# Eight weight buffers at eight different remainders modulo 512 bytes

## The chip, the core and the metric

The kernel runs on one core of a Trainium2 chip. The metric is the device time of one execution in microseconds. The profile comes from one profiled execution of the same program. Engines are named as the profile names them: PE is TensorE (PEld its weight loads), DVE is VectorE, ACT is ScalarE, POOL is GpSimd, SP is SyncE, which issues most of the DMAs.

## The reference

Two transformer layers over one sequence of 512 tokens of width 1024, all in float32. Layer 0 mixes tokens with dilated sliding-window attention, layer 1 with multi-head latent attention; each mixer is followed by a squared-ReLU MLP of hidden width 4096:

```python
for i in range(DEPTH):                       # DEPTH = 2
    h = rms_norm(x, norm_mix[i])
    if i % 2 == 0:                           # three head groups, dilations 1, 4, 16
        y = dilated_mixer(h, a_w_qkv[0], a_q_gain[0], a_k_gain[0], a_w_o[0])
    else:                                    # low-rank q and kv, rotary part of 64
        y = mla_mixer(h, b_w_in[0], ..., b_w_o[0])
    x = x + y
    h = rms_norm(x, norm_ffn[i])
    a = relu(h @ ffn_w1[i])                  # 1024 x 4096
    x = x + (a * a) @ ffn_w2[i]              # 4096 x 1024
```

Nearly all of the arithmetic is in the products of activations with weight matrices: the q, k and v projection (1024 x 9216), the two output projections, and the four MLP matrices.

## The kernel before, in words

The products run on PE in the type `float32r`, in three parts that keep float32's precision. A weight block of 128 partitions x 1024 elements comes from HBM into a float32 tile (`raw`, `wqs` or a block `b`). ACT writes its rounded half `whi`, DVE writes the remainder `wlo` = block - `whi`. Activations are split in the same way, into `hT`, `asp`, `Ssp` or `cT`. Each product is then high x high, high x low and low x high, accumulated in one PSUM bank.

`whi` and `wlo` are tiles of `[128, 2, 512]`, 4096 bytes in each partition. They come from the pool `wp`, which holds four of each (and three of `raw`), and are given out in turn. A `whi` is free again when its last matmul has read it, so ACT's next split can wait for PE, DVE's for ACT, and PE's next matmul for DVE. Three places make them:

- `load_unit` (L150) for the projections and the first MLP matrix: L157 on ACT, L158 on DVE. Its matmuls are at L185. In the mixers and the projections the halves are the moving operand, 512, 448 or 384 columns wide, and the activations the stationary one; in the first MLP matrix (`up`, L873) slices of 128 columns of the halves are the stationary operand, and the activations `hT_f0` and `hT_f1` move.
- the `split_w` of `v_phase` (L403) for most of the v projection, a 2 x 2 block product with seven products: L406 on ACT, L407 on DVE, matmuls at L421, the halves moving, 384 columns wide.
- the `split_w` of `wino` (L792) for the second MLP matrix, again with seven products: L795 on ACT, L796 on DVE, matmuls at L852, the halves moving, 512 columns wide.

The latent mixer's projections of q and kv (L1032) use `load_unit` too.

Pools are laid out one behind the other in each partition. In the program before, every large tile, and with it each of the eight weight halves, `raw`, `wqs`, `hT`, `asp` and the rest, starts at an address with the remainder 192 modulo 512. Slices of 128 float32 columns are 512 bytes long and keep that remainder.

The order of instructions on each engine comes from the Tile scheduler, which orders the program as it is built.

Of the kernel before, what the change touches and what calls it, by code (L numbers as in the profile page):

```python
# [10 lines left out]
F32 = mybir.dt.float32  # L11
F32R = mybir.dt.float32r
# [5 lines left out]
P = 128  # L18
# [69 lines left out]
def encoder_kernel(ctx: ExitStack, tc: tile.TileContext, x, norm_mix, norm_ffn, a_w_qkv, a_q_gain, a_k_gain,  # L88
# [3 lines left out]
    V, A, G, PE = nc.vector, nc.scalar, nc.gpsimd, nc.tensor  # L92
# [3 lines left out]
    def nm(s):  # L96
        uid[0] += 1
        return f"{s}_{uid[0]}"
# [6 lines left out]
    wp = ctx.enter_context(tc.tile_pool(name="wp", bufs=4))  # L105
    gp = ctx.enter_context(tc.tile_pool(name="gp", bufs=1))
# [13 lines left out]
    ident = ck[:, C_ID:C_ID + P]  # L120
    A.activation(warm, nhalf[:, 0:1], AF.Exp)

    def transpose(o, i):
        PE.transpose(o, i, ident)  # L124

# [13 lines left out]
    def load_raw(src, nk, dims, n):  # L139
        raw = wp.tile([P, 2, 512], F32, tag="raw", name=nm("raw"), bufs=3)  # L140
        dst = raw[:, :nk, :n]
        if dims:
            dst = dst.rearrange("p k (t c) -> p k t c", t=dims)
            for k in range(nk):
                nc.sync.dma_start(dst[:, k], src[:, k])
        else:
            nc.sync.dma_start(dst, src)
        return raw

    def load_unit(src, nk, dims, n, home=None, raw=None):  # L150

        if raw is None:
            raw = load_raw(src, nk, dims, n)
        if home is None:
            home = [wp.tile([P, 2, 512], F32R, tag=t, name=nm(t)) for t in ("whi", "wlo")]
        hi, lo = home
        A.activation(hi[:, :nk, :n], raw[:, :nk, :n], AF.Copy)  # L157
        V.tensor_tensor(lo[:, :nk, :n], raw[:, :nk, :n], hi[:, :nk, :n].bitcast(F32), op=ALU.subtract)  # L158
        return hi, lo, nk
# [54 lines left out]
    def norm_tile(r, src, gain_b, hT, pool, xn_bufs=2, xn_tag="xn"):  # L214

        ss = st.tile([P, 8], F32, tag="nss", name=nm("nss"))
        xn = pool.tile([P, D], F32, tag=xn_tag, name=nm("xn"), bufs=xn_bufs)
        mean_square(xn, src, D, ss[:, 0:1])
        rs = rstd_of(ss[:, 0:1], 1, EPS, "nrs")
        V.scalar_tensor_tensor(xn, src, rs, gain_b, op0=ALU.mult, op1=ALU.mult)  # L220
        for half in range(2):
            tp = tp_p.tile([P, 512], F32, tag="tp", name=nm("tp"))
            for j in range(4):
                transpose(tp[:, j * P:(j + 1) * P], xn[:, (half * 4 + j) * P:(half * 4 + j + 1) * P])
            hi = hT[:, half * 4:half * 4 + 4, 0, r * P:(r + 1) * P]
            lo = hT[:, half * 4:half * 4 + 4, 1, r * P:(r + 1) * P]
            tv = tp.rearrange("p (k t) -> p k t", k=4)
            A.activation(hi, tv, AF.Copy)
            V.tensor_tensor(lo, tv, hi.bitcast(F32), op=ALU.subtract)
# [22 lines left out]
    VH = 3 * DH  # L252
# [54 lines left out]
    def v_phase(vp):  # L307
# [93 lines left out]
        A_OF = {1: of_hT(0, 0), 2: of_hT(0, 1), 4: of_hT(1, 1), 5: of_S(1), 6: of_S(2), 7: of_S(3), 3: of_S(4)}  # L401

        def split_w(x):  # L403
            hi = wp.tile([P, 2, 512], F32R, tag="whi", name=nm("whi"))[:, :, :VH]
            lo = wp.tile([P, 2, 512], F32R, tag="wlo", name=nm("wlo"))[:, :, :VH]
            A.activation(hi, x, AF.Copy)  # L406
            V.tensor_tensor(lo, x, hi.bitcast(F32), op=ALU.subtract)  # L407
            return hi, lo

        def split(p, w, u):  # L410
            parts[p, u] = split_w(w[:, 2 * u:2 * u + 2])
# [343 lines left out]
    def split_a(x, pool):  # L755
        t = pool.tile([P, 4, 2, 256], F32R, tag="asp", name=nm("asp"), bufs=4)
        A.activation(t[:, :, 0], x, AF.Copy)
        V.tensor_tensor(t[:, :, 1], x, t[:, :, 0].bitcast(F32), op=ALU.subtract)
        return t

    def wino(tag, Aq, w, wqs, pool, resid, done=None):

        v = w.rearrange("(k p) c -> p k c", p=P)  # L770
        S = {}
        slots = SLOTS[tag % 4]

        def fetch(slot, key, add=False):

            ki, ni = key
            for u in range(2):
                t = wqs[:, 2 * slot + u]
                src = v[:, 4 * ki + 2 * u:4 * ki + 2 * u + 2, 512 * ni:512 * ni + 512]
                if add:  # L780
                    marks["sum"] = nc.gpsimd.dma_start(t, src, accum_op=ALU.add).ins  # L781
                else:
                    nc.sync.dma_start(t, src)
            return [wqs[:, 2 * slot + u] for u in range(2)]

        def stmp(name, x, y, op):
            if name not in S:
                S[name] = pool.tile([P, 4, 256], F32, tag="S", name=nm("S"), bufs=2)
            V.tensor_tensor(S[name], x, y, op=op)
            return S[name]  # L790

        def split_w(x):  # L792
            hi = wp.tile([P, 2, 512], F32R, tag="whi", name=nm("whi"))
            lo = wp.tile([P, 2, 512], F32R, tag="wlo", name=nm("wlo"))
            A.activation(hi, x, AF.Copy)  # L795
            V.tensor_tensor(lo, x, hi.bitcast(F32), op=ALU.subtract)  # L796
            return hi, lo

        sT, s1, s3, s7 = slots
        b1 = fetch(s1, (0, 0))  # L800
        fetch(sT, (0, 0))
        bT = fetch(sT, (0, 1), add=True)
        b3 = fetch(s3, (1, 1))
        fetch(s7, (0, 1))
        b7 = fetch(s7, (1, 1), add=True)

        def operands(p):
            if p == 5:
                return stmp("c", Aq(1, 0), Aq(1, 1), ALU.subtract), bT
            if p == 1:  # L810
                return Aq(0, 0), b1
            if p == 3:
                stmp("d", S["c"], Aq(0, 0), ALU.subtract)
                return stmp("c", S["d"], Aq(0, 1), ALU.add), b3
            if p == 6:
                return S["d"], fetch(sT, (1, 1), add=True)
            if p == 7:
                return stmp("c", Aq(0, 0), Aq(1, 0), ALU.subtract), b7
            if p == 2:
                return Aq(0, 1), fetch(s1, (1, 0))  # L820
            return Aq(1, 1), fetch(sT, (1, 0), add=True)

        def put(i, n, op, banks):
            for t in range(2):
                sl = resid[:, 2 * i + t, 512 * n:512 * n + 512]
                V.tensor_tensor(sl, sl, banks[t], op=op)  # L826
                if done is not None and p in (2, 4, 6, 7):
                    done(2 * i + t, n)

        banks = {}  # L830
        for p, chain, first, (i, n, op) in ORDER if done is None else ORDER_LAST:
            a, wq = operands(p)
            at = split_a(a, pool)
            if first:
                pl, tg = {"a": (sc_p, "sc"), "b": (tp_p, "tp"), "d": (tp_p, "tp")}[chain]
                if done is not None and chain == "d":
                    pl, tg = acc_p, "acc"
                banks[chain] = [pl.tile([P, 512], F32, tag=tg, name=nm(tg)) for _ in range(2)]
            bk = banks[chain]

            tail = done is not None and p in (7, 4)
            parts = {}
            for u, t in ((0, 0), (1, 0), (0, 1), (1, 1)) if tail else ((0, 0), (0, 1), (1, 0), (1, 1)):
                if u not in parts:
                    parts[u] = split_w(wq[u])
                hi, lo = parts[u]
                for j in range(2):
                    k = 2 * u + j
                    ah = at[:, k, 0, t * P:(t + 1) * P]
                    al = at[:, k, 1, t * P:(t + 1) * P]  # L850
                    for i_, (lt, rt) in enumerate(((ah, hi), (ah, lo), (al, hi))):
                        PE.matmul(bk[t], lhsT=lt, rhs=rt[:, j], start=(first and k == 0 and i_ == 0),  # L852
                                  stop=(k == 3 and i_ == 2), skip_group_check=True)
            put(i, n, op, bk)
# [96 lines left out]
    if True:  # L951
        with tc.tile_pool(name="bpool", bufs=1, reuse_waits="tile") as bp, \
# [208 lines left out]
            for s_ in range(HB * NT + lag):  # L1161
                p, c = divmod(s_, 8)
# [64 lines left out]
```

## Time and profile before

| what | value |
|---|---|
| time, median of 2 runs (1428.57 and 1428.98) | 1428.78 us |
| span of the profiled execution, first to last instruction | 1425.8 us |
| granted PE clock over the span | 1.000 |
| PE busy | 1394.0 us (98%) |
| PEld busy | 1183.8 us (83%) |
| DVE busy | 939.6 us (66%) |
| ACT busy | 740.5 us (52%) |
| POOL busy | 217.2 us (15%) |
| mean DMA rate | 130 GB/s |

The timed runs are 3.0 us above the profiled span: that lies around the first and the last instruction. In a group's row, busy time counts overlapping instructions once, and the mean of one is the length of one from its start to its modelled end. Matmuls follow each other faster than that mean, since one starts before the one ahead of it has ended; the distance of their starts is read from a run of them with its count and length, in the chain of waits.

### The profile page before, as it was taken

How to read it: one execution, taken by the hardware profiler on the slowest of the kernel's cores; microseconds unless marked ns; L12 is line 12 of the kernel's file. 1: busy time of each engine (PE TensorE's matmuls, PEld its weight loads, DVE VectorE, ACT ScalarE, POOL GpSimd, SP SyncE). 2: the span in 40 equal slices, each digit the busy share in tenths (PEclk: the TensorE clock that was granted, in tenths of full speed). 3: DMA queues.
4: the chain of work that ended last, by engine and by line, in shares of the span. 5: the costliest groups of instructions: out<-in, count | busy, mean ns of one | idle time of the engine just before them, and what ended most of it. 6: DMA issues, size and time to landing. Idle time of an engine off the chain costs nothing.

```text
span 1425.8 us, 19234 instructions
## 1 busy us (share of the span) xinstructions
PE 1394.0 (98%) x7044; PEld 1183.8 (83%) x7044; DVE 939.6 (66%) x1497; ACT 740.5 (52%) x1594; POOL 217.2 (15%) x240
## 2 busy tenths in 40 slices
PE   7999999999999999999999999999999999999998
PEld 7999888988888988888888887777768888888886
DVE  6886768676886754465564759788745365575647
ACT  6554656464564623553545446677633553544543
POOL 1110212021112001020010203433201020020201
PEclk9999999999999999999999999999999999999999
DMA  9535222322322335668493844200115658394835
GB/s 323 166 134 168 75 87 87 107 89 75 118 61 77 121 134 195 174 133 222 116 233 99 206 120 91 82 31 30 44 40 163 183 127 231 93 234 128 192 90 118
DMA packets 121086, 185.25 MB, mean 130 GB/s; under 512 B 8416, under 2 KB 58336, under 8 KB 120992
## 3 DMA queue, kind: packets, MB, share of 16 engines
q1 hardware_dynamic: 101808, 144.96, 31.6%
q0 software_dynamic: 19184, 39.07, 15.2%
q8 instruction: 55, 0.90, 0.3%
q14 instruction: 39, 0.32, 0.1%
HBM read 176.13 MB, written 7.86 MB: 129 GB/s over the span
## 4 chain that ended last, share of the span: by engine, by line
PE 89%; DVE 6%; ACT 2%; issue 1%; DMA 1%; POOL 0%; SPq 0%; DVEq 0%; ACTq 0%; POOLq 0%
PE acc L185 51%; PE sc L852 11%; PE tp L852 7%; PE tp L124 4%; PE sc L421 3%; PE acc L1138 1%; PE sc L1032 1%; PE acc L1114 1%; PE tp L421 1%; DVE wlo L796 1%; PE sco L701 1%; PE sc L587 1%; PE acc L421 1%; PE sco L697 1%; DVE wlo L407 1%
## 5 line engine op out<-in xcount | busy, mean ns | idle before, releaser
L185 PE MATMUL acc<-whi,hT 128*128 128x512 f32 (+2 forms) x1216 | 384.2, 390 | 2.2 <-ACT hT L739 1.3
L185 PE MATMUL acc<-hT_f,whi 128*128 128x512 f32 (+1 forms) x1152 | 318.7, 366 | 1.7 <-DVE resid L915 1.2
L158 DVE TENSOR_TENSOR wlo<-raw,whi 128x1024 fp32r<-128x1024 f32 (+3 forms) x146 | 172.4, 1189 | 180.2 <-ACT whi L157 179.9
L185 PEld LDWEIGHTS acc<-whi,hT 128*128 128x128 f32 x1216 | 225.4, 188 | 42.0 <-ACT hT L739 1.9
L185 PEld LDWEIGHTS acc<-hT_f,whi 128*128 128x128 f32 x1152 | 208.1, 189 | 37.4 <-DVE resid L915 1.6
L185 PE MATMUL acc<-wlo,hT 128*128 128x512 f32 (+2 forms) x608 | 235.9, 388 | 0.0
L157 ACT ACTIVATE whi<-raw 128x1024 fp32r<-128x1024 f32 (+3 forms) x146 | 149.7, 1031 | 161.5 <-PE acc L185 64.1
L796 DVE TENSOR_TENSOR wlo<-wqs,whi 128x1024 fp32r<-128x1024 f32 x112 | 137.9, 1232 | 113.4 <-ACT whi L795 113.4
L185 PE MATMUL acc<-hT_f,wlo 128*128 128x512 f32 (+1 forms) x576 | 204.9, 366 | 0.0
L795 ACT ACTIVATE whi<-wqs 128x1024 fp32r<-128x1024 f32 x112 | 118.8, 1061 | 161.3 <-PE acc L185 65.8
L852 PE MATMUL sc<-whi,asp 128*128 128x512 f32 x512 | 164.9, 390 | 0.8 <-DVE resid L826 0.7
L781 POOL DMA_DIRECT2D wqs<-in_ffn_w_dram x64 | 77.6, 1344 | 546.1 <-DVE wlo L796 362.4
L185 PEld LDWEIGHTS acc<-wlo,hT 128*128 128x128 f32 x608 | 114.4, 188 | 18.7 <-issue 0.2
L185 PEld LDWEIGHTS acc<-hT_f,wlo 128*128 128x128 f32 x576 | 108.5, 189 | 17.4
L852 PE MATMUL tp<-whi,asp 128*128 128x512 f32 x352 | 112.2, 390 | 1.8 <-DVE resid L826 1.8
L852 PEld LDWEIGHTS sc<-whi,asp 128*128 128x128 f32 x512 | 96.1, 188 | 21.4 <-issue 1.5
L132 POOL TENSOR_TENSOR qrs<-rs_v,nhalf 128x4 f32<-128x4 f32 x48 | 58.7, 1228 | 288.8 <-DVE rs_v L129 239.7
L852 PE MATMUL sc<-wlo,asp 128*128 128x512 f32 x256 | 99.6, 389 | 0.0
L137 ACT ACTIVATE junk<-acc 128x128 f32<-128x128 f32 x192 | 53.0, 276 | 56.4 <-PE acc L185 51.4
L852 PEld LDWEIGHTS tp<-whi,asp 128*128 128x128 f32 x352 | 66.1, 188 | 16.4 <-DVE resid L826 2.7
L852 PE MATMUL tp<-wlo,asp 128*128 128x512 f32 x176 | 68.2, 389 | 0.0
L295 ACT ACTIVATE qkT<-tp 128x512 f32<-128x512 f32 x48 | 35.8, 765 | 51.2 <-PE tp L124 50.9
(231 smaller groups left out, 2185.3 us busy)
## 6 DMA issues: line engine op xcount, KB each, us to landing
wqs<-in_ffn_w_dram SPq DMA_DIRECT2D x80, 512.0 KB, 5.1
raw<-in_ffn_w_dram SPq DMA_DIRECT2D x64, 512.0 KB, 4.5
wqs<-in_ffn_w_dram POOLq DMA_DIRECT2D x64, 512.0 KB, 7.5
raw<-in_a_w_qkv_dram SPq DMA_DIRECT2D x96, 256.0 KB, 3.1
b<-in_a_w_qkv_dram SPq DMA_DIRECT2D x24, 384.0 KB, 5.7
vall<-vo POOLq DMA_DIRECT2D x24, 192.0 KB, 2.2
raw<-in_a_w_o_dram SPq DMA_DIRECT2D x8, 512.0 KB, 3.8
raw<-in_b_w_o_dram SPq DMA_DIRECT2D x8, 512.0 KB, 3.7
```

The source lines that it names most:

```text
L124: PE.transpose(o, i, ident)
L132: G.tensor_tensor(out, v[:, :n], nhalf[:, :n], op=ALU.pow)
L137: A.activation(junk, x, AF.Square, scale=1.0 / math.sqrt(dim), accum_out=out)
L157: A.activation(hi[:, :nk, :n], raw[:, :nk, :n], AF.Copy)
L158: V.tensor_tensor(lo[:, :nk, :n], raw[:, :nk, :n], hi[:, :nk, :n].bitcast(F32), op=ALU.subtract)
L185: PE.matmul(accs[o][:, oc], lhsT=lt, rhs=rt, start=(kt == 0 and p_i == 0 and hv == 0), stop=(kt == total - 1 and p_i == 2), skip_group_che ...
L295: A.activation(dst, tv, AF.Copy)
L421: PE.matmul(banks[t][:, :VH], lhsT=lt, rhs=rt[:, j], start=(first and k == 0 and i_ == 0), stop=(k == 3 and i_ == 2), skip_group_check=True)
L781: marks["sum"] = nc.gpsimd.dma_start(t, src, accum_op=ALU.add).ins
L795: A.activation(hi, x, AF.Copy)
L796: V.tensor_tensor(lo, x, hi.bitcast(F32), op=ALU.subtract)
L852: PE.matmul(bk[t], lhsT=lt, rhs=rt[:, j], start=(first and k == 0 and i_ == 0), stop=(k == 3 and i_ == 2), skip_group_check=True)
```

## The change

Each of the eight buffers becomes 96 bytes longer: `wbuf` takes a tile of 1048 elements (4192 bytes) from the same pool and hands out 1024 of them as `[128, 2, 512]`, from element 0 for `whi` and from element 4 (16 bytes) for `wlo`. A new tile `lead` of 256 bytes in the pool `gp`, which lies behind `wp`, is set to zero once; with the eight times 96 bytes it makes 1024 bytes, by which every tile behind them moves, so that these keep their remainder modulo 512. `raw`, `ck`, `hT` and `wqs` lie ahead of the buffers and stay where they are.

In the built program the four `whi` start at the remainders 192, 288, 384 and 480, the four `wlo` at 80, 176, 272 and 368, and all other large tiles at 192 as before. All eight are multiples of 16 bytes; two of them (192 and 384) are multiples of 64, the other six are not.

```diff
+    lead = gp.tile([P, 64], F32, tag="lead", name="lead")
+    V.memset(lead, 0.0)
+
+    def wbuf(tag):
+        n0 = 4 if tag == "wlo" else 0
+        t = wp.tile([P, 1048], F32R, tag=tag, name=nm(tag))
+        return t[:, n0:n0 + 1024].rearrange("p (k n) -> p k n", k=2)
...
         if home is None:
-            home = [wp.tile([P, 2, 512], F32R, tag=t, name=nm(t)) for t in ("whi", "wlo")]
+            home = [wbuf(t) for t in ("whi", "wlo")]
...
         def split_w(x):
-            hi = wp.tile([P, 2, 512], F32R, tag="whi", name=nm("whi"))[:, :, :VH]
-            lo = wp.tile([P, 2, 512], F32R, tag="wlo", name=nm("wlo"))[:, :, :VH]
+            hi = wbuf("whi")[:, :, :VH]
+            lo = wbuf("wlo")[:, :, :VH]
...
         def split_w(x):
-            hi = wp.tile([P, 2, 512], F32R, tag="whi", name=nm("whi"))
-            lo = wp.tile([P, 2, 512], F32R, tag="wlo", name=nm("wlo"))
+            hi = wbuf("whi")
+            lo = wbuf("wlo")
```

On PE, ACT, POOL and SP the same instructions stand in the same order before and after. On DVE one instruction is new. These are the first rows of DVE's program before (`nhalf` is a constant, `nss` the first tile's sum of squares, `b` the first weight block of the v projection):

```order
L1222 UNCONDITIONAL_BRANCH
L117 MEMSET nhalf 128x8
L129 TENSOR_SCALAR rs_v_158<-nss_156 128x1
L361 SCALAR_TENSOR_TENSOR xn_110<-xts,nrs_160,g_mix_3_119 128x1024
L407 TENSOR_TENSOR wlo_164<-b_4_122,whi_163 128x2x384
```

And these of the changed program, whose line numbers are 8 higher behind the new lines:

```order
L1230 UNCONDITIONAL_BRANCH
L117 MEMSET nhalf 128x8
L124 MEMSET lead 128x64
L137 TENSOR_SCALAR rs_v_160<-nss_158 128x1
L369 SCALAR_TENSOR_TENSOR xn_112<-xts,nrs_162,g_mix_3_121 128x1024
L415 TENSOR_TENSOR wlo_166<-b_4_124,whi_165 128x2x384
```

The zeroing of `lead` stands between the constant and the first instruction that waits for data; nothing reads `lead`.

## The prediction

> **What bounds the kernel now.** I read the page's totals first, then a table by stage, the chain of waits, and the groups of instructions by line. The totals say that PE is never long without work:
>
> ```profile
> span 1425.8 us, 19234 instructions
> PE 1394.0 (98%) x7044; PEld 1183.8 (83%) x7044; DVE 939.6 (66%) x1497; ACT 740.5 (52%) x1594; POOL 217.2 (15%) x240
> ```
>
> The table of busy times by stretch shows where the 2% lie. Its columns are length, PE, PEld, DVE, ACT, POOL (busy us and count), the granted PE clock, the DMA share and GB/s. The rows are the dilated mixer behind its v projection, most of the first MLP, the latent mixer, most of the second MLP, and the end.
>
> ```profile
> 135.00:540.00 405.00, 403.26 (x2238) 348.59 (x2237) 285.22 (x564) 215.24 (x720) 59.25 (x49) 1.00 0.31 96
> ...
> 575.00:860.00 285.00, 285.00 (x1265) 236.04 (x1264) 168.88 (x165) 142.77 (x164) 31.50 (x26) 1.00 0.65 161
> 860.00:1085.00 225.00, 214.51 (x1051) 168.74 (x1051) 169.06 (x414) 135.05 (x392) 62.57 (x90) 1.00 0.17 48
> ...
> 1100.00:1380.00 280.00, 280.00 (x1298) 234.56 (x1298) 153.74 (x150) 133.28 (x154) 32.51 (x27) 1.00 0.67 168
> 1380.00:1425.70 45.70, 40.81 (x178) 32.85 (x176) 32.77 (x35) 20.35 (x23) 4.82 (x4) 1.00 0.40 92
> ```
>
> In 565 us of MLP PE has no idle time at all, at full clock, with DVE busy for 169 of 285 us. There only a shorter distance between matmuls can gain time, and only a longer one, or a split of weights late by more than its slack, can lose it. Busy PE is not yet PE at its best, so I need that distance. The chain of waits has long unbroken runs (start, length, line, count); the first here is of the v projection's matmuls, 384 columns wide, the second of the first MLP's, 512 wide:
>
> ```profile
> 113.65 8.50 PE sc L421 x49
> ...
> 742.95 40.57 PE acc L185 x179
> ```
>
> That is 40.57 / 179 = 226.6 ns for 512 columns and 8.50 / 49 = 173.5 ns for 384. The difference of 53.1 ns over 128 columns is 0.415 ns a column, so 512 columns take 212.5 ns and some 14 ns stand beside them in each matmul, the same at both widths. These 14 ns are the only thing in the bound stretches that a change of addresses could take away.
>
> **What the change touches.** Most matmuls that read a weight half are in these eight groups of the page (count, then busy us and mean ns of one; the mean runs to the modelled end, so it is above the distance):
>
> ```profile
> L185 PE MATMUL acc<-whi,hT 128*128 128x512 f32 (+2 forms) x1216 | 384.2, 390 | 2.2 <-ACT hT L739 1.3
> L185 PE MATMUL acc<-hT_f,whi 128*128 128x512 f32 (+1 forms) x1152 | 318.7, 366 | 1.7 <-DVE resid L915 1.2
> ...
> L185 PE MATMUL acc<-wlo,hT 128*128 128x512 f32 (+2 forms) x608 | 235.9, 388 | 0.0
> ...
> L185 PE MATMUL acc<-hT_f,wlo 128*128 128x512 f32 (+1 forms) x576 | 204.9, 366 | 0.0
> ...
> L852 PE MATMUL sc<-whi,asp 128*128 128x512 f32 x512 | 164.9, 390 | 0.8 <-DVE resid L826 0.7
> ...
> L852 PE MATMUL tp<-whi,asp 128*128 128x512 f32 x352 | 112.2, 390 | 1.8 <-DVE resid L826 1.8
> ...
> L852 PE MATMUL sc<-wlo,asp 128*128 128x512 f32 x256 | 99.6, 389 | 0.0
> ...
> L852 PE MATMUL tp<-wlo,asp 128*128 128x512 f32 x176 | 68.2, 389 | 0.0
> ```
>
> Together 1216 + 1152 + 608 + 576 + 512 + 352 + 256 + 176 = 4848 matmuls. One buffer of eight keeps the remainder 192, so about 4848 x 7/8 = 4242 read a moved one.
>
> **PE.** What the move is worth to a matmul is not in the trace directly, since before it every large operand starts at 192. Three things bear on it. First, the same 389 to 390 ns stand for halves that move (L852) and, by line and shape, for halves that are loaded as weights (`hT_f`):
>
> ```profile
> L185 PE MATMUL acc<-whi,hT 128*128 128x512 f32 x1024 | 331.8, 397 | 2.2 <-ACT hT L739 1.3 <-ACT hT L1140 0.7
> L185 PE MATMUL acc<-hT_f,whi 128*128 128x512 f32 x896 | 270.8, 389 | 0.0
> ...
> L580 PE MATMUL sc<-qkT 128*128 128x128 f32 x64 | 12.4, 275 | 0.0
> ...
> L576 PE MATMUL sc<-qkT 128*128 128x128 f32 x64 | 12.3, 274 | 0.0
> ```
>
> Second, the last two rows are the nearest thing to the change. Both use slices of the same tile `qkT` for both operands; at L576 the moving keys start at the same remainder as the queries, at L580 each matmul takes two pieces of 64 keys of which one starts 256 bytes further modulo 512. They take 274 and 275 ns. Third, were PE's two reads to meet at every step of a weight load of 128 columns, the price would be 128 steps of 0.415 ns, 53 ns, and not 14. I take 0 for the gain. Its end is 4242 x 14 ns = 59 us, if all of the 14 ns were such meetings. The loss I take at 0 too. Its end comes from the largest difference between rows of the same shape, 397 against 389 ns in the mixers: 8 ns x 4242 = 34 us, if a start off a multiple of 64 bytes, which six of the eight have, cost as much as whatever lies behind that difference.
>
> The Trainium skill has a figure against me here: "TensorE: Matmul & The Clock Gate", section "Wait — 56ns, not 53.3ns?", gives a fixed cost of about 2.5 ns for each warm matmul beside its columns. This trace disagrees, with 14 ns. If only that page's 2.5 ns were unavoidable and the rest came from addresses, an estimate of 4242 x 11.5 ns = 49 us would be gained, and the sum would be 1380 us.
>
> **DVE and ACT.** They write and read the halves when splitting. If two reads at the same remainder cost DVE anything, an operation with both inputs in SBUF at 192 would be longer than one with its first input in PSUM. They stand side by side in the groups by line and shape, 683 and 685 ns (L285 and L277):
>
> ```profile
> L158 DVE TENSOR_TENSOR wlo<-raw,whi 128x1024 fp32r<-128x1024 f32 x128 | 155.5, 1224 | 177.3 <-ACT whi L157 177.0
> ...
> L277 DVE TENSOR_TENSOR t<-acc,cosg 128x512 f32<-128x512 f32 x48 | 32.9, 685 | 12.0 <-ACT junk L137 7.2 <-PE tp L124 4.6
> L285 DVE TENSOR_TENSOR t<-t,t 128x512 f32<-128x512 f32 x48 | 32.6, 683 | 0.1
> ```
>
> The same view for ACT, and, for the line that splits `wqs` on DVE, its shortest, median and longest instruction:
>
> ```profile
> L795 ACT ACTIVATE whi<-wqs 128x1024 fp32r<-128x1024 f32 x112 | 118.8, 1061 | 161.3 <-PE acc L185 65.8 <-PE tp L852 48.7 <-PE sc L852 26.0
> ...
> L892 ACT ACTIVATE a<-a 128x512 f32<-128x512 f32 x64 | 40.4, 632 | 2.0
> ...
> L796 DVE TENSOR_TENSOR wlo<-wqs,whi x112: 1217/1226/1539, 606.7 to 1412.2; 128x1024 fp32r<-128x1024 f32 x112
> ```
>
> From 512 to 1024 elements DVE goes from 683 to 1224 ns, 1.06 ns for each added element, ACT from 632 to 1061, 0.84 ns; neither slope leaves room for a meeting at every element. So 0 here too. L796 gives the other end: if every split on DVE took the longest 1539 ns in place of 1226, the factor would be 1.26. In the MLPs PE's full stretches above cover it: some 60 splits x 0.31 us = 19 us more on a DVE that is idle for 116 of 285 us. What counts is the part of the chain that runs through splits:
>
> ```profile
> PE acc L185 51%; PE sc L852 11%; PE tp L852 7%; PE tp L124 4%; PE sc L421 3%; PE acc L1138 1%; PE sc L1032 1%; PE acc L1114 1%; PE tp L421 1%; DVE wlo L796 1%; PE sco L701 1%; PE sc L587 1%; PE acc L421 1%; PE sco L697 1%; DVE wlo L407 1%
> ```
>
> Two shares of 1% are about 28 us, and 26% of that is 7 us, at the ends of the v projection and of the MLPs. POOL's accumulating loads wait for L796 as well and would come as much later; they have the same cover.
>
> **The new instruction, and the shift.** The nearest row for zeroing 128x64 is the constant's 128x8, 0.07 us, and DVE then waits for data until 5.65:
>
> ```profile
> 0.80 0.07 DVE L117 MEMSET nhalf<- 128x8 f32 x1 [0.80 <-PEq L1210]
> ...
> 5.65 0.15 DVE L129 TENSOR_SCALAR rs_v<-nss 128x1 f32<-128x1 f32 x1 [4.78 <-ACT xn L137]
> ```
>
> It is free; without that wait it would cost about its own length, 0.1 us. All tiles behind the buffers lie 1024 bytes further at the same remainder; nothing in the trace distinguishes the two places: 0. No DMA reads or writes a weight half, so no transfer changes its shape, and no wait is added to any engine.
>
> **Sum.** 1425.8 us span + 0 (PE) + 0 (splits) + 0 (new instruction, shift) = 1425.8 us, and with the 3.0 us by which the timed runs (1428.57 and 1428.98) lie above the span, 1428.8 us.
>
> **Rivals.**
> *Meetings resolved (faster).* PE's read of moving columns and its weight load now walk in step through addresses of equal remainder; apart, the 14 ns shrink. In full this gives 1428.8 - 59 = 1370 us; 2% is reached from 28.6 us / 4242 = 6.7 ns a matmul. For it speaks that the 14 ns are there at both widths, as a weight load of constant size would have it; against it L576 beside L580, and that 14 ns are no multiple of such a load. A small form of it is possible in the mixers alone: 4.2 us if half of the 8 ns between 397 and 389 went from the 1024 matmuls of that row; 1424.6 us. Chances: 3% for the large form, 5% for the small one.
> *Starts off a multiple of 64 bytes (slower).* Each read of a displaced half takes one fetch more, on PE's moving side at L852 and in the mixers, on its weight side at `up`. At 8 ns this is 1428.8 + 34 = 1463 us; it decides, at +2%, from 6.7 ns. For it speaks only that no row of before has such a start; against it, that all new starts are still multiples of 16 bytes, and that a fetch more for a run of 2048 bytes should cost some single steps of 0.415 ns: two of them on 4242 matmuls are 3.5 us, 1432.3 us. The Trainium skill ("SBUF — State Buffer", section "Specifications (TRN2)") gives lines of 16 bytes, by which no read here touches one line more. No row here shows the size of a line. Chances: 4% for over 2%, 6% for the small form.
> *Slower splits.* Up to 7 us, 1436 us, as worked out above; 2%.
> *The change does not do what it says.* If the padded tiles were rounded up by the allocator to a multiple of 512 bytes, the `whi` would not be displaced; the built addresses speak against it, and the time would be the forecast's. 1%, counted with the forecast.
>
> **Numbers.** The forecast has 80%: 1428.8 us, with its own range of about 1427 to 1431, since the two runs differ by 0.4 us. The small forms (5%, 6%) reach to 1424.6 and 1432.3. The range of 1424.5 to 1433 holds these and leaves out the large forms (3% and 4%) and part of the slower splits. A difference of 2%, 28.6 us, is what I count as faster or slower; all but the two large forms lie within it, so faster 3%, same 93%, slower 4%.
>
> **What would show it.** Right: runs of about 226.6 ns a matmul at L185 and 173.5 ns at L421 (line numbers 8 higher), 389 ns in the groups of L852, 1224 to 1232 ns for the splits on DVE, and no idle PE in the two MLP stretches. The first rival would show as a shorter distance in just those runs; the second as a longer one, with the groups that read no half (L576, L124) as they were. The forecast would be wrong if 14 ns change by over 2 ns (4242 x 2 ns = 8.5 us).

## The result and the profile after

The changed kernel takes 1445.06 us (1443.68 and 1446.43) against 1428.78 us: the ratio is 1.0115, with a 95% interval of 1.0098 to 1.0131. It is slower by 16 us, clear of the measurement and outside the range of the prediction. By the bound of 2% it counts as no change, but the forecast was that nothing moves at all.

The page's totals after:

```profile
span 1441.9 us, 19235 instructions
PE 1411.2 (98%) x7044; PEld 1183.0 (82%) x7044; DVE 939.6 (65%) x1498; ACT 740.0 (51%) x1594; POOL 217.2 (15%) x240
```

The table by stretch of after for two windows that lie wholly in the MLPs (length, PE, PEld, DVE, ACT, POOL as busy us and count, PE clock, DMA share, GB/s):

```profile
600.00:850.00 250.00, 250.00 (x1081) 202.55 (x1080) 143.26 (x141) 118.16 (x135) 29.09 (x24) 1.00 0.66 163
1150.00:1375.00 225.00, 225.00 (x974) 182.47 (x973) 134.93 (x135) 107.50 (x121) 29.10 (x24) 1.00 0.66 163
```

The same two windows of before:

```profile
600.00:850.00 250.00, 250.00 (x1105) 207.01 (x1104) 148.64 (x147) 123.09 (x140) 29.09 (x24) 1.00 0.65 162
1150.00:1375.00 225.00, 225.00 (x995) 186.36 (x994) 131.86 (x132) 106.68 (x120) 29.11 (x24) 1.00 0.68 166
```

In both kernels PE has no idle time there, at full clock. But in the same 250 us PE starts 1081 matmuls in place of 1105. DVE and ACT are as busy as before over the span (939.6 and 740.0 us). So the time went into the matmuls themselves. The groups by line and shape of after show by how much (busy us, mean ns of one; the line numbers are 8 higher than before):

```profile
L193 PE MATMUL acc<-whi,hT 128*128 128x512 f32 x1024 | 335.0, 400 | 2.2 <-ACT hT L747 1.3 <-ACT hT L1148 0.7
L193 PE MATMUL acc<-hT_f,whi 128*128 128x512 f32 x896 | 275.0, 394 | 0.0
L193 PE MATMUL acc<-wlo,hT 128*128 128x512 f32 x512 | 204.0, 399 | 0.0
L193 PE MATMUL acc<-hT_f,wlo 128*128 128x512 f32 x448 | 171.1, 393 | 0.0
L860 PE MATMUL sc<-whi,asp 128*128 128x512 f32 x512 | 167.4, 394 | 0.5 <-DVE resid L834 0.5
L860 PE MATMUL tp<-whi,asp 128*128 128x512 f32 x352 | 113.8, 394 | 1.1 <-DVE resid L834 1.1
L860 PE MATMUL sc<-wlo,asp 128*128 128x512 f32 x256 | 100.7, 393 | 0.0
...
L588 PE MATMUL sc<-qkT 128*128 128x128 f32 x64 | 12.4, 275 | 0.0
```

Two rows that the prediction did not need are, before:

```profile
L185 PE MATMUL acc<-wlo,hT 128*128 128x512 f32 x512 | 202.7, 396 | 0.0
L185 PE MATMUL acc<-hT_f,wlo 128*128 128x512 f32 x448 | 169.1, 389 | 0.0
```

The first MLP matrix's means went from 389 to 394 and 393, the second's from 390 and 389 to 394 and 393, those of the mixers and projections from 397 and 396 to 400 and 399. The keys that read no weight half (L588, L580 before) stay at 275. The second matrix has one more group of 176, which the page gives with 389 before and 393 after. Put together: 896 x 5 + 448 x 4 + (512 + 352) x 4 + (256 + 176) x 4 ns = 11.5 us in the MLPs, and 1024 x 3 + 512 x 3 ns = 4.6 us in the mixers. The sum is 16.1 us, and the spans differ by 1441.9 - 1425.8 = 16.1 us. Means in whole ns make the agreement closer than it deserves: 0.5 ns on the 4176 matmuls of these groups are already 2 us. The smaller groups moved both ways (384 columns mostly longer by 1 to 4 ns, 256 columns shorter by 2) and nearly cancel; no other large term is needed.

The chain of waits shows the distance of the starts. One run each of the v projection (384 columns), the second MLP matrix and the first (512 columns), after:

```profile
113.71 8.58 PE sc L429 x49
...
652.87 5.59 PE sc L860 x24
...
667.02 41.51 PE acc L193 x179
```

41.51 / 179 = 231.9 ns in place of 226.6, and 8.58 / 49 = 175.1 in place of 173.5. Runs of 24 in the second matrix took 5.44 us (226.7 ns) before and take 5.52 to 5.59 us now (230 to 233 ns).

The splits did not change, on DVE and on ACT:

```profile
L166 DVE TENSOR_TENSOR wlo<-raw,whi 128x1024 fp32r<-128x1024 f32 x128 | 155.5, 1224 | 182.2 <-ACT whi L165 178.9 <-PE acc L193 2.8
```

```profile
L803 ACT ACTIVATE whi<-wqs 128x1024 fp32r<-128x1024 f32 x112 | 118.8, 1061 | 162.4 <-PE acc L193 67.2 <-PE tp L860 55.4 <-PE sc L860 28.1
```

The new instruction stands in the timeline where it was expected (start, length):

```profile
0.85 0.11 DVE L124 MEMSET lead<- 128x64 f32 x1
```

### The profile page after: what moved, and what is told of

Same layout as the page of the kernel before. It is cut to its first block, busy times and chain, and to the rows that moved or that the text cites. A ratio compares the mean times of both kernels' runs of the same rounds, so it can differ in the third digit from the quotient of the medians.

```text
span 1441.9 us, 19235 instructions
## 1 busy us (share of the span) xinstructions
PE 1411.2 (98%) x7044; PEld 1183.0 (82%) x7044; DVE 939.6 (65%) x1498; ACT 740.0 (51%) x1594; POOL 217.2 (15%) x240
## 4 chain that ended last, share of the span: by engine, by line
PE 89%; DVE 6%; ACT 2%; issue 1%; DMA 1%; POOL 1%; SPq 0%; DVEq 0%; ACTq 0%; POOLq 0%
PE acc L193 52%; PE sc L860 11%; PE tp L860 7%; PE tp L132 4%; PE sc L429 3%; PE tp L429 1%; PE acc L1146 1%; PE sc L1040 1%; PE acc L1122 1%; DVE wlo L804 1%; PE sco L709 1%; PE sc L595 1%; PE sco L705 1%; PE acc L429 1%; PE sc L1122 1%
## 5 line engine op out<-in xcount | busy, mean ns | idle before, releaser
L193 PE MATMUL acc<-hT_f,whi 128*128 128x512 f32 (+1 forms) x1152 | 322.4, 369 | 1.5 <-DVE resid L923 1.0
L193 PEld LDWEIGHTS acc<-hT_f,whi 128*128 128x128 f32 x1152 | 207.6, 188 | 41.5 <-DVE resid L923 1.4
L803 ACT ACTIVATE whi<-wqs 128x1024 fp32r<-128x1024 f32 x112 | 118.8, 1061 | 162.4 <-PE acc L193 67.2
```

Of the source, the lines that this page charges most:

```text
L193: PE.matmul(accs[o][:, oc], lhsT=lt, rhs=rt, start=(kt == 0 and p_i == 0 and hv == 0), stop=(kt == total - 1 and p_i == 2), skip_group_che ...
```

## The experiments

Every kernel below has the same instructions in the same order on each engine, apart from one to three zeroings of unused tiles; only addresses differ. "Displaced by d" means that the weight halves start d bytes past the remainder of their partners in the matmul (`hT`, `hT_f0`, `hT_f1`, `asp`, `Ssp`, `cT`), which is 192 modulo 512 unless something else is said. Distances come from the chain of waits: a run of 179 matmuls of the first MLP matrix, in which the halves are loaded as weights, and runs of 24 of the second, in which they move.

### The change again, the shift alone, one other remainder, multiples of 64

The first set asked whether the change is the cause at all, and which part of it. `e1_again` is the changed kernel.

> The changed kernel as it is, once more and in turns with the kernel before. Three theories stand. Rhythm: weight loads and moving reads of successive matmuls fall into a fixed rhythm (226.6 ns for 512 columns) when all weight halves start at one remainder, and find none when the start changes from one matmul to the next (231.6 ns in the trace of after). Line: a start off a multiple of 64 bytes costs some steps in each read. Place: not the remainders but the shift of the other tiles by 1024 bytes, or the moment of the runs, made the difference. Rhythm and line: 16 us above before again (ratio 1.011), 231 to 232 ns in the MLPs. Place, if it was the moment: ratio 1.000, 226.6 ns.

```diff
 e2_shift: halves of 4096 bytes, all the shift in lead
-    lead = gp.tile([P, 64], F32, tag="lead", name="lead")
+    lead = gp.tile([P, 256], F32, tag="lead", name="lead")
-        t = wp.tile([P, 1048], F32R, tag=tag, name=nm(tag))
+        t = wp.tile([P, 1024], F32R, tag=tag, name=nm(tag))        # and n0 = 0
```

> All eight halves of 4096 bytes at remainder 192 as before; only the tile lead, of 1024 bytes, is there, so that everything behind the halves is shifted by 1024 bytes as in the change. Rhythm and line: the time of before, ratio 1.000, 226.6 ns for 512 columns. Place, if it was the shift: ratio 1.011, 231 to 232 ns.

```diff
 e3_all288: as e2_shift, with 96 of the 1024 bytes ahead of the halves
+    pre = pp.tile([P, 24], F32, tag="pre", name="pre")             # pool pp lies between raw and the halves
+    lead = gp.tile([P, 232], F32, tag="lead", name="lead")
```

> All eight halves at one other remainder, 288, which is off a multiple of 64; the other tiles as in the change. Rhythm: the same for all halves, so the rhythm stays, ratio 1.000, 226.6 ns, or another fixed distance. Line: eight of eight starts displaced in place of six, 16 x 8/6 = 22 us above before, ratio 1.015, 233 ns. Place (shift): ratio 1.011.

```diff
 e5_mult64: a step of 64 bytes from half to half
-        t = wp.tile([P, 1048], F32R, tag=tag, name=nm(tag))
+        t = wp.tile([P, 1040], F32R, tag=tag, name=nm(tag))        # n0 = 0, lead of 512 bytes
```

> Eight halves at eight different remainders, all multiples of 64 (192, 256, 320, 384, 448, 0, 64, 128); the other tiles as in the change. Rhythm: no rhythm, ratio 1.011, 231 to 232 ns. Line: no start displaced, ratio 1.000, 226.6 ns. Place (shift): ratio 1.011.

| kernel | ratio (95%) | first matrix, 179 | second matrix, 24 |
|---|---|---|---|
| e1_again | 1.0113 (1.0096 to 1.0130) | 41.4 to 41.5 us, 231 to 232 ns | 5.52 to 5.59 us |
| e2_shift | 1.0000 (0.9990 to 1.0009) | 40.57 us, 226.6 ns | 5.44 us, 226.7 ns |
| e3_all288 | 1.0175 (1.0160 to 1.0190) | 41.92 us, 234.2 ns | 5.59 to 5.60 us, 233 ns |
| e5_mult64 | 1.0114 (1.0098 to 1.0129) | 41.4 to 41.5 us, 231 to 232 ns | 5.53 to 5.59 us |

The effect repeats, and the shift alone has none: "place" falls. The multiples of 64 are as slow as the change, so starts off a multiple of 64 are not the cause: "line" falls as well, although its 1.015 for `e3_all288` came nearest to the 1.0175 measured there. That run surprised the "rhythm" theory in its first form. All halves had one start, and yet the kernel was slower than with eight. A rhythm was there, but a longer one, as the chain of `e3_all288` shows:

```profile
658.09 5.59 PE sc L864 x24
672.31 41.92 PE acc L197 x179
```

So it is not enough that successive halves start alike. What was left was the place of the half, by itself or against that of its partner.

### The difference between what moves and what is loaded

PE's weight load for the next matmul runs beside the present matmul. Before, in a stretch of the timeline (start, length), the load and the matmul begin together and the load ends 0.03 to 0.04 us ahead of the next start:

```profile
701.76 0.39 PE L852 MATMUL sc<-whi,asp 128*128 128x512 f32 x1
701.76 0.19 PEld L852 LDWEIGHTS sc<-wlo,asp 128*128 128x128 f32 x1
...
701.98 0.39 PE L852 MATMUL sc<-wlo,asp 128*128 128x512 f32 x1
```

So the two instructions overlap for most of a distance, and the addresses that they read can differ by a constant, which the second set varies. `e6_d64`, `e7_d128` and `e8_d256` are `e3_all288` with another length of `pre`. `e9_world64` displaces everything together:

```diff
 e6_d64, e7_d128, e8_d256
-    pre = pp.tile([P, 24], F32, tag="pre", name="pre")
+    pre = pp.tile([P, 16], F32, tag="pre", name="pre")             # 32 and 64 in the other two
 e9_world64: the kernel before, with 64 bytes ahead of the first large tile
+    lead = cpool.tile([P, 16], F32, name="lead")
     ck = cpool.tile([P, C_KEEP], F32, name="ck")
```

> All eight halves at remainder 256, 64 bytes past the partners (hT, hT_f, asp, Ssp), which stay at 192. The theory is now that the difference of remainders between what moves and what is loaded as weights at the same time sets the rhythm. Relative: a fixed pattern as with the difference of 96 bytes, 228 to 235 ns for 512 columns in both MLP parts, ratio 1.005 to 1.018. Rival, absolute: the place of a read in 512 bytes counts by itself; then the result is the same as in the kernel where everything is at 256.

> All eight halves at remainder 320, the partners at 192, a difference of 128 bytes. Relative, with 512 bytes as the period: a pattern of its own, 228 to 235 ns. If the period were 128 bytes or a divisor of it: 226.6 ns and the time of before.

> All eight halves at remainder 448, the partners at 192, a difference of 256 bytes. Relative, with 512 bytes as the period: a pattern of its own, 228 to 235 ns; with 256 bytes as the period: 226.6 ns and the time of before.

> The kernel before with 64 bytes put ahead of everything but two constants, so that halves, partners, raw tiles and all the rest start at 256 and every difference is 0. Relative: 226.6 ns and the time of before, ratio 1.000, whatever the run with the halves alone at 256 gives. Absolute: the same as that run.

| kernel | displaced by | ratio (95%) | first matrix, 179 | second matrix, 24 |
|---|---|---|---|---|
| e6_d64 | 64 | 1.0083 (1.0053 to 1.0112) | 41.77 us, 233.4 ns | 5.49 to 5.60 us |
| e7_d128 | 128 | 1.0143 (1.0113 to 1.0172) | 41.60 us, 232.4 ns | 5.57 to 5.60 us |
| e8_d256 | 256 | 0.9996 (0.9985 to 1.0007) | 40.57 us, 226.6 ns | 5.44 us |
| e9_world64 | 0, all at 256 | 0.9996 (0.9985 to 1.0008) | 40.57 us, 226.6 ns | 5.44 us |

The rows for the last two are the same to the last digit. The run with the halves 256 bytes past their partners:

```profile
646.98 5.44 PE sc L864 x24
660.81 40.57 PE acc L197 x179
```

and the one in which everything starts at 256:

```profile
648.25 5.44 PE sc L854 x24
662.08 40.57 PE acc L187 x179
```

Halves at 256 cost 12 us when their partners are at 192 (`e6_d64`) and nothing when those are at 256 too (`e9_world64`). So the difference counts, not the place. And it counts modulo 256 bytes, not 512: a displacement of 256 is none.

### Two remainders, one displaced half of three, the engines beside PE, and 32 bytes

```diff
 e10_lo256, e11_lo96: whi as before, a pad of 256 or 96 bytes between the whi and the wlo
+    wl = ctx.enter_context(tc.tile_pool(name="wl", bufs=4))         # behind a pool with the pad
-        t = wp.tile([P, 1024], F32R, tag=tag, name=nm(tag))
+        t = (wl if tag == "wlo" else wp).tile([P, 1024], F32R, tag=tag, name=nm(tag))
 e12_raw96: 96 bytes ahead of raw, 416 between raw and the halves, 512 behind them
+    pre0 = pq.tile([P, 24], F32, tag="pre0", name="pre0")
+    pre = pp.tile([P, 104], F32, tag="pre", name="pre")
 e13_d32: as e3_all288
+    pre = pp.tile([P, 8], F32, tag="pre", name="pre")
```

> whi at 192 as before, wlo at 448: two different remainders modulo 512 that are equal modulo 256, and the address of the halves steps by 256 from one matmul to the next. If the differences count modulo 256 and not modulo 512: 226.6 ns, ratio 1.000. If any change of the remainder modulo 512 between successive matmuls breaks the rhythm: 229 ns or more, ratio above 1.005.

> whi at 192 as before, wlo at 288: one of three matmuls reads a displaced half. If only the read of the displaced half is stretched: a third of what all halves at 288 cost, 25/3 = 8 us, ratio 1.006, with the other two thirds of the matmuls at 226.6 ns. If the phase that one displaced read leaves behind also stretches the ones after it (rhythm): more than a third, up to the 1.011 of the change.

> Halves and partners at 192 as before, the raw tiles alone at 288, so that ACT and DVE read and write at a difference of 96 in every split of load_unit (mixers, projections and first MLP matrix) and PE's two reads keep the difference 0. If PE's two reads meet each other: 226.6 ns everywhere, ratio 1.000. If PE is held up by the accesses of ACT and DVE, whose remainders against each other the change also moved: 231 ns or more in the first MLP matrix and the mixers, ratio 1.007 to 1.011, and 226.6 ns in the second MLP matrix.

> All eight halves at 224, 32 bytes past the partners. With the differences 64, 96 and 128 giving ratios of 1.008, 1.018 and 1.014, no order is seen; rhythm: a pattern of its own, 227 to 235 ns, ratio 1.001 to 1.018. If only differences of 64 bytes or more count: 226.6 ns, ratio 1.000.

| kernel | ratio (95%) | first matrix, 179 | second matrix, 24 |
|---|---|---|---|
| e10_lo256 | 1.0002 (0.9991 to 1.0013) | 40.57 us | 5.44 us |
| e11_lo96 | 1.0114 (1.0080 to 1.0149) | 41.57 us, 232.2 ns | 5.55 us, 231.3 ns |
| e12_raw96 | 1.0000 (0.9989 to 1.0012) | 40.57 us | 5.44 us |
| e13_d32 | 1.0153 (1.0122 to 1.0185) | 41.76 us, 233.3 ns | 5.60 us, 233.3 ns |

`e10_lo256` alternates between two remainders modulo 512 in successive matmuls and costs nothing; that settles 256 as the period of everything seen here. In `e11_lo96` one matmul of three reads a displaced half, and the price is not a third of that of `e3_all288` but nearly two thirds (1.0114 against 1.0175). The matmuls that read the undisplaced `whi` became longer too, as the groups by shape of that run show; before they were at 389 and 390:

```profile
L197 PE MATMUL acc<-hT_f,whi 128*128 128x512 f32 x896 | 275.4, 394 | 0.0
...
L864 PE MATMUL sc<-whi,asp 128*128 128x512 f32 x512 | 167.4, 394 | 0.5 <-DVE resid L838 0.5
```

In the second matrix (L864) what is loaded is always `asp`, so a matmul of `whi` has the difference 0 both to its own weights and to those that are loaded beside it, and its group is longer all the same. So a matmul whose own two reads fit is stretched by what its neighbours left behind. That fits the changed kernel, in which no buffer stands out, the one still at 192 included: the distances in its second matrix, grouped by the four buffers that take turns, average 231 to 232 ns in each group.

`e12_raw96` speaks against the accesses of ACT and DVE: the splits of `load_unit` read and write there at a difference of 96 bytes, and nothing happens. A trace settles it. In `e3_all288` there is a stretch without any instruction on DVE, ACT or POOL (columns as in the tables by stretch above):

```profile
683.10:685.80 2.70, 2.70 (x13) 2.14 (x12) 0.00 (x0) 0.00 (x0) 0.00 (x0) 1.00 0.65 189
```

PE's timeline there, its first and its last matmul of a low half:

```profile
682.91 0.40 PE L197 MATMUL acc<-hT_f,wlo 128*128 128x512 f32 x1
...
685.72 0.39 PE L197 MATMUL acc<-hT_f,wlo 128*128 128x512 f32 x1
```

From the first to the last of these starts there are 12 matmuls in 2.81 us, 234 ns each, as far apart as in the rest. DMAs were under way there (share 0.65). Another stretch of `e3_all288`, in the latent mixer, has none, with the chain's run of matmuls in it:

```profile
1088.05:1099.15 11.10, 11.10 (x49) 8.95 (x48) 4.62 (x7) 2.30 (x4) 1.12 (x2) 1.00 0.00 0
```

```profile
1087.92 11.20 PE acc L197 x48
```

and the same stretch of before:

```profile
1070.45:1081.25 10.80, 10.80 (x49) 8.97 (x48) 4.60 (x7) 2.30 (x4) 1.12 (x2) 1.00 0.00 0
```

```profile
1070.35 10.88 PE acc L185 x48
```

Without a DMA it is 11.20 / 48 = 233.3 ns against 10.88 / 48 = 226.7, the same difference. So neither the other engines nor the transfers are needed for it. What is left are PE's own two reads; no edit here touches a tile in PSUM, where PE writes.

### The sign of the difference

In `e6_d64` the halves stood 64 bytes past their partners. The weights were then 64 past what moved in the first MLP matrix, and 64 short of it in the second. `e15_d192` exchanges the two, since 192 is -64 modulo 256:

```diff
-    pre = pp.tile([P, 16], F32, tag="pre", name="pre")
+    pre = pp.tile([P, 48], F32, tag="pre", name="pre")
```

> All eight halves at 384, 192 bytes past the partners, which modulo 256 is 64 bytes ahead of them. What is loaded as weights then stands to what moves as +64 where the halves move (second MLP matrix) and as -64 where they are the weights (first MLP matrix): the two roles of the run with the halves alone at 256, exchanged. If the difference modulo 256 between the two reads sets the rhythm, the two distances there, 233.3 ns (first matrix) and 230.8 ns (second matrix, mean), change places: 231 in the first, 233 in the second. If the amount of the displacement counts without its sign or only on one operand, they stay as they are there, or take a value of their own. Ratio 1.007 to 1.012 either way.

The ratio was 1.0115 (1.0086 to 1.0145). Runs of `e15_d192`:

```profile
653.39 5.60 PE sc L864 x24
667.59 40.99 PE acc L197 x179
```

and of `e6_d64`:

```profile
649.34 5.49 PE sc L864 x24
663.38 41.77 PE acc L197 x179
```

The first matrix went from 233.4 to 229.0 ns, the second from 228.8 ns, which most of its runs of 24 have in `e6_d64`, to 233.3 in all of them. The places changed as expected, with 229.0 ns where 231 was expected, so the sign of the difference counts: weights 64 bytes past what moves give 233.3 ns in either role. The other value is not equally sharp. It is 229.0 ns in one role and 228.8 ns in the other, but a part of the runs of 24 in `e6_d64` settled at 5.60 us (233.3 ns): at one difference there can be more than one pattern that lasts.

## Why the prediction was wrong

**What bounds it** held: PE without idle time in the MLPs at full clock, and only the distance of the matmuls can move the time. The 226.6 and 173.5 ns were the right numbers to look at, and they are what changed.

**The term for PE was wrong.** It was taken as 0 and measures 16 us, the sum of the groups above. The prediction looked in two directions, a gain from PE's two reads at equal remainders and a loss from starts off a multiple of 64. For the 0 of the loss it gave no reason of its own, only that this one way to it was unlikely. The loss that came belongs to the pair of reads in which the gain was sought, with the sign reversed: of the differences tried, 0, 32, 64, 96, 128 and 192 modulo 256, none gave 512 columns a distance below the 226.6 ns of the difference 0.

The three reasons given for 0 did not show what they were taken for. That 389 ns stood for halves that move and for halves loaded as weights only said that both roles had the difference 0. L576 beside L580 was meant as the nearest row to the change; its displacement was 256 bytes, and `e8_d256` and `e10_lo256` show that just this displacement is none. And the argument from 53 ns a load supposed a meeting at every step of the load; the real price is 2 to 8 ns.

The Trainium skill's figure of 2.5 ns beside the columns ("TensorE: Matmul & The Clock Gate", section "Wait — 56ns, not 53.3ns?") is not reached at any of these addresses: the 14 ns at difference 0 are the least that was seen at 512 columns. They are not a fixed cost either: at 256 columns a difference of 64 leaves some 8 ns beside the columns (114.2 - 256 x 0.415 ns, from the last section). What they consist of stays open.

**The bound held, but mostly by luck.** The end taken from 397 against 389 ns, 8 ns x 4242 = 34 us, held the result, and the range of 1424.5 to 1433 left it out, because 8 ns was given 4% only. But most of these 8 ns are something else. A matmul right behind matmuls of another kind is longer, as the first one here, behind four transposes:

```profile
200.67 0.60 PE L124 MATMUL tp<-ck,t 128*128 128x128 f32 x4
201.03 0.47 PE L185 MATMUL acc<-whi,hT 128*128 128x512 f32 x1
201.34 0.39 PE L185 MATMUL acc<-wlo,hT 128*128 128x512 f32 x1
```

Of the 1024 + 512 matmuls of the two mixer groups in the kernel before, 110 stand in such a place, with a mean of 474 ns; the other 1426 have 391 ns. So only about 2 of the 8 ns are left for what bears on the change, a rhythm that is lost behind a group of transposes and found again some matmuls later. PE's timeline at one such place (start, length):

```profile
186.58 0.60 PE L124 MATMUL tp<-ck,t 128*128 128x128 f32 x4
186.93 0.71 PE L185 MATMUL acc<-whi,hT 128*128 128x512 f32 x2
187.48 0.39 PE L185 MATMUL acc<-wlo,hT 128*128 128x512 f32 x1
187.71 0.86 PE L185 MATMUL acc<-whi,hT 128*128 128x512 f32 x3
188.41 0.39 PE L185 MATMUL acc<-wlo,hT 128*128 128x512 f32 x1
188.64 0.62 PE L185 MATMUL acc<-whi,hT 128*128 128x512 f32 x2
189.09 0.39 PE L185 MATMUL acc<-wlo,hT 128*128 128x512 f32 x1
```

Behind the transposes two matmuls take 0.55 us and the next three 0.70 us (233 ns each); then 0.68 us pass from 188.41 to 189.09 for three (227 ns). In a stream that was otherwise constant to a nanosecond, this was the trace's sign, before the change, that the distance depends on what came before.

**Two counts were off,** without weight for the outcome. Each product reads `whi` twice and `wlo` once, and the buffer that keeps 192 is a `whi`, so 3232 x 3/4 + 1616 = 4040 matmuls read a moved half, not 4242. And DVE makes 28 + 50 = 78 splits in the 285 us of the first MLP's row, not some 60; at 0.31 us each these are 24 us, still less than the 116 us of idle time.

**DVE, ACT, the new instruction and the shift** were right at 0: the splits keep 1224 and 1061 ns, the zeroing took 0.11 us in DVE's wait, and `e2_shift` gives 1.0000.

**The rivals.** "Meetings resolved" had the right place, PE's two reads, and the wrong sign. "Starts off a multiple of 64 bytes" had the right sign and would have given a time of this size at 4 ns a matmul, but its mechanism is refuted by `e5_mult64` and `e6_d64`, in which all starts are multiples of 64 and the time is longer all the same.

**What stays open.** The runs show that the distance follows the signed difference of the two addresses modulo 256, that history carries over (so that one difference can have two distances, as in `e6_d64`), and that neither the other engines nor DMAs are needed for it. That both reads go to the same piece of memory with a period of 256 bytes in a partition is the plain reading, but only argued. Which part of the weight load meets which part of the moving read was not tried, nor differences that are no multiple of 32, apart from those in the changed kernel.

## What to carry to other kernels

Where a kernel is bound by a dense stream of matmuls, the addresses of the two operands are part of its speed: here 512 columns took 226.6 ns when moving and stationary operand started at the same place modulo 256 bytes, and 229 to 234 ns at every other multiple of 32 that was tried, up to 1.8% of the time. Tiles whose sizes are multiples of 256 bytes, laid one behind the other, keep this by themselves; one odd small tile or a padded buffer between two operands is enough to lose it. To see it in a trace, divide the length of an unbroken run of equal matmuls by its count, and compare with another placement. One value throughout is no proof of a good one: `e3_all288` had 234.2 ns in its runs of 179, as steady as the 226.6 ns of before. In the changed kernel runs of 24 varied from 5.52 to 5.59 us, where before all took 5.44.

## What was not expected of the hardware

- The distance of matmuls depends on the difference of the two addresses modulo 256 bytes, with its sign, and on nothing else about the addresses that was tried: 233.3 ns at +64, 229 ns at -64 (233.3 in some runs of 24), 232.4 ns at 128, 226.6 ns at 0 and at 256.
- The effect is not bound to the displaced matmuls: with one of three displaced, the other two were stretched as well (389 and 390 to 394 ns).
- For 256 columns it goes the other way. The first groups of the first MLP matrix are 384 matmuls of 256 columns. In the chain a run of 24 of them takes 2.87 to 2.88 us wherever the difference is 0 and 2.74 to 2.86 us in every other kernel here. Before, and with the halves displaced by 64 (`e6_d64`), 120.0 and 114.2 ns each:

```profile
555.76 2.88 PE acc L185 x24
```

```profile
557.09 2.74 PE acc L197 x24
```

The larger of the two groups, in the same two runs:

```profile
L185 PE MATMUL acc<-hT_f,whi 128*128 128x256 f32 x256 | 48.0, 287 | 1.7 <-DVE resid L915 1.2 <-ACT hT_f L228 0.5
```

```profile
L197 PE MATMUL acc<-hT_f,whi 128*128 128x256 f32 x256 | 45.8, 281 | 1.6 <-DVE resid L927 1.1 <-ACT hT_f L240 0.5
```

The group's mean can be compared only where the clock was full: in `e1_again`, `e5_mult64`, `e7_d128`, `e10_lo256`, `e11_lo96` and `e12_raw96` the granted clock fell to a half for 3.4 us within this group in the second layer, and its mean is 288 to 292 ns, at a difference of 0 (`e10_lo256`, `e12_raw96`) as well.

Six nanoseconds on 384 matmuls would be 2.3 us, 0.16%, for a kernel that displaces the halves in this group alone. It was not run.
